# Two mixing layers: the heads' projections first, then pooling and gating, with values, gates and pooled part as one 400-column moving operand

## The chip, the cores and the metric

The kernel runs on one core of one Trainium2 chip. The time is device microseconds of one execution; three executions of the kernel before give a median of 1850.83 us. Smaller is better. All arithmetic is float32 in accuracy: every large product is made of three matmuls on float32r operands (high part by high part, high by low, low by high).

## The reference, cut to what matters

Two blocks of two layers each act on 256 tokens of 1024 channels. The change concerns the mixing half of the two layers of the second block, where `l` is 0 and 1:

```
h = rms_norm_2(x, norm_mix_pre[l])
z = h @ w_in[l]
za, zq, zkv, zg, zc, zd = split(z)          # 512, 256, 384, 12, 512, 256 columns
y_conv = conformer_conv(za, ...)            # gate, 31 taps along time, layer norm, silu
y_nsa  = nsa_attention(zq, zkv, sigmoid(zg), ...)   # 4 heads: compressed, selected, window branches
y_sgu  = spatial_gating(zc, ...)            # gelu, layer norm of v, 128x128 mixing along time, u * f
y_pool = multiscale_pool(zd, ...)           # running means minus the value, a small projection
y = concat(y_conv, y_nsa, y_sgu, y_pool) @ w_out[l]
x = x + rms_norm_2(y, norm_mix_post[l])
```

The four parts are independent of each other until `w_out`, whose 1024 rows fall into four groups of 256: rows 0 for the convolution, 1 for the heads, 2 for the gating, 3 for the pooled part.

## The kernel before, in words

One Python function writes the instruction stream of each engine in a fixed order. While it does so it keeps a model clock for each engine; small generators (one for each chain such as the pooled part or a pair of heads) are advanced between stretches of matmuls, and each next instruction of a chain is written when the model says that its inputs will be there. On the chip each engine takes its instructions in the order written. So what is written behind a matmul that waits, waits too.

Weights come as chunks of 1 MB or 0.5 MB (512 KB is one unit, 128 x 1024) over SyncE's queue in the order of `_plan()`, into four raw buffers (`wraw`). ScalarE casts each unit to `whi`, VectorE subtracts to make `wlo`; there are seven unit buffers. `MIX_ORDER` (line 57) is the order in which a mixing layer's projections run, and also the order of its chunks in `_weights`. `MIX_ROWS` (line 58) is the order of the four groups of rows of `w_out`.

In `mix` (line 2113) the order is: `begin`, which multiplies the first two pairs of units (`ag0`, `ag1`, the convolution's input) by the not yet scaled input while the norm is made, after which `make_h` writes the scaled input `hh`, `hl` in eight chunks of 128 channels (order 0, 2, 1, 3, 4, 6, 5, 7); then

- `v` (48 matmuls with tokens as stationary operand and 256 weight columns moving) and `u` (48 matmuls of the other form), the two halves of the gating, each followed by a gelu on ScalarE; a generator `sgu_gen` makes the layer norm, the mixing along time and the product;
- `conv`, which waits until `gated_input` has written the convolution's second input half, and then makes 18 of its 31 taps on TensorE, while 31 taps of the first half and 13 of the second run on VectorE as fillers, wherever VectorE's model clock is less than 1 us behind;
- `cvf` and `kk` (24 matmuls each: compressed keys and values; the other keys), `cw1` (the compression), `q` (48 matmuls);
- `cvt` (48: values and 12 gate columns, padded with 116 zero columns to 256) and `zd` (48: the pooled part), then `pool_gen`;
- `mm4`, which takes four neighbouring PSUM banks, and the four groups of rows, 48 matmuls each, in the order 2, 3, 0, 1. Before each group `rows` waits until its part is in `oh`, `ol`.

Two generators `nsa_heads` (t = 0, 1) each do two heads: logits, masked maximum on VectorE, exponentials on ScalarE, scaling on VectorE, transposes on TensorE, copies to `PT` on ScalarE, value products. Both use the same `P` and `PT` buffers. `self.busy` keeps the second from its logits until the first has its value products written. `tokens` (line 841) and `unit` (line 832) are the two forms of projection. After the fourth group `post` makes the norm, and the convolutional feed-forward layer (`ffn2`) follows.

Of the kernel before, what the change touches and what calls it, by code (L numbers as in the profile page):

```python
# [24 lines left out]
F32 = mybir.dt.float32  # L25
# [4 lines left out]
OP = mybir.AluOpType  # L30
# [23 lines left out]

FOX_ORDER = '0 1 f v0 2 3 v1 4 5 v2 6 7 v3'.split()

MIX_ORDER = 'v u conv cvf kk cw1 q cvt zd'.split()
MIX_ROWS = (2, 3, 0, 1)


DIL_TOKENS = ((3, 3, 3), (3, 3, 3), (3, 3, 3), (1, 1, 3))
# [6 lines left out]
def _weights(seg):  # L68

    kind, l, j = seg  # L70
    out = []
    if kind in ("ffn", "ffn2"):
        if kind == "ffn":
            g, u, d = (("ffn_w_gate", (l, j)), 0), (("ffn_w_up", (l, j)), 0), ("ffn_w_down", (l, j))
        else:
            g, u, d = (("ffn_up_2", (l,)), 0), (("ffn_up_2", (l,)), 2816), ("ffn_down_2", (l,))
        for t in range(FT):
            out.append((("pair", g[0], g[1] + t * 128, u[0], u[1] + t * 128), 2))
            if t % 2 and t > 4:
                out.append((("row", d, (t // 2 - 2) * 256), 2))  # L80
        for half in range(2):
            out.append((("last", d, half), 2))
    elif kind == "fox":
        w = ("fox_w_in", (0,))
        for i in FOX_ORDER:
            out.append((("one", w, 3072, 16), 1) if i == "f" else
                       (("tok", w, 2048 + int(i[1]) * 256) if i[0] == "v" else
                        ("pair", w, int(i) * 128, w, 1024 + int(i) * 128), 2))
        for c in range(4):
            out.append((("row", ("fox_w_out", (0,)), c * 256), 2))  # L90
    elif kind == "dil":
        w = ("dil_w_in", (0,))
        for c in range(4):
            toks = [(("tok", w, (g * 3 + 2) * 1024 + c * 256), 2) for g in range(3)]
            qk = [(("pair", w, o, w, o + 1024), 2) for e in range(2) for g in range(3) for o in (g * 3072 + (2 * c + e) * 128,)]
            early = 0 if c else 2
            out += qk[:early] + toks[:DIL_TOKENS[c][0]]
            for e in range(2):
                out += qk[max(3 * e, early):3 * e + 3]
                out += toks[DIL_TOKENS[c][e]:DIL_TOKENS[c][e + 1]]  # L100
        for c in range(4):
            out.append((("row", ("dil_w_out", (0,)), c * 256), 2))
    elif kind == "mix":
        for which in ["ag0", "ag1"] + [w for w in MIX_ORDER if w != "conv"]:
            n = 1 if which in ("cvf", "kk") else 2
            out.append((("cw1", l) if which == "cw1" else ("mixt" if which in ("v", "cvt", "zd") else "mix", l, which), n))
        for c in MIX_ROWS:
            out.append((("row", ("w_out_2", (l,)), c * 256), 2))
    return out
# [75 lines left out]
def _chunk_data(key, a):  # L185

    kind = key[0]
    tok = lambda w: np.concatenate([_kxn(w[:512]), _kxn(w[512:])], axis=1)
    get = lambda m: a[m[0]][m[1]]
    if kind == "mod":  # L190
        _, l, b = key
        return a["mod_w"][l][:, b * 128:(b + 2) * 128].T.reshape(2, 128, 1024).transpose(1, 0, 2).reshape(128, -1)
    if kind == "pair":
        _, m0, c0, m1, c1 = key
        return np.concatenate([_kxn(get(m0)[:, c0:c0 + 128]), _kxn(get(m1)[:, c1:c1 + 128])], axis=1)
    if kind == "wave":
        _, i, part = key
        r = slice(i * 256, i * 256 + 256)
        gu = [get(("ffn_w_" + n, (0, 0)))[r] for n in ("gate", "up")]
        return np.concatenate([_kxn(np.concatenate([m[:, t * 128:t * 128 + 256] for m in gu], axis=1))  # L200
                               for t in ((0, 2), (4, 6))[part]], axis=1)
    if kind == "one":
        _, m, c0, n = key
        w = get(m)[:, c0:c0 + n]
        return _kxn(np.concatenate([w, np.zeros((w.shape[0], 128 - n), np.float32)], axis=1))
    if kind == "tok":
        _, m, c0 = key
        return tok(get(m)[:, c0:c0 + 256])
    if kind == "row":
        _, m, r0 = key  # L210
        w = get(m)[r0:r0 + 256]
        return np.concatenate([_kxn(w[:, :512]), _kxn(w[:, 512:])], axis=1)
    if kind == "last":
        _, m, half = key
        w = get(m)[-512:, half * 512:half * 512 + 512]
        return np.concatenate([_kxn(w[:256]), _kxn(w[256:])], axis=1)
    if kind in ("mix", "mixt"):
        _, l, which = key
        cols = _mix_columns(which)
        real = [c for c in cols if c is not None]  # L220
        w = a["w_in_2"][l][:, real]
        if len(real) < len(cols):
            w = np.concatenate([w, np.zeros((1024, len(cols) - len(real)), np.float32)], axis=1)
        if kind == "mixt":
            return tok(w)
        return np.concatenate([_kxn(w[:, i:i + 128]) for i in range(0, w.shape[1], 128)], axis=1)
    _, l = key
    return np.concatenate([a[n][l].reshape(32, 64, 64).transpose(1, 0, 2).reshape(64, -1)
                           for n in ("nsa_ck_w1_2", "nsa_cv_w1_2")], axis=0)
# [163 lines left out]
NRAW = 4  # L393
NU = 7
UNIT = 1024


def parted(ap):
# [153 lines left out]
class Stream:  # L552
# [42 lines left out]
    def step(self, limit, later=None):  # L595


        i, u = self.at
# [12 lines left out]
        if key[0] == "mod":  # L611
            col = key[1] * 72 + key[2] + u
            nc.vector.tensor_tensor_reduce(src, src, k.cb, 1.0, 0.0, OP.mult, OP.add, k.modr[:, col:col + 1])
        else:
            if self.live >= limit:
                return False
            self.live += 1
            hi = k.whi.tile([128, UNIT], F32R, name="whi", bufs=NU)
            lo = k.whi.tile([128, UNIT], F32R, name="wlo", bufs=NU)
            nc.scalar.copy(hi, src)  # L620
            low = lambda: nc.vector.tensor_tensor(lo, src, hi.bitcast(F32), op=OP.subtract)
            if later is None:
                low()
            else:
                later.append(low)
            self.units.append((key, u, hi, lo))
# [13 lines left out]
    def get(self, *check):  # L640
        find = lambda: next((i for i, x in enumerate(self.units) if x[0][:len(check)] == check), None)
        while find() is None:
            assert self.step(NU), ("stuck", self.at)
        key, u, hi, lo = self.units[find()]
        del self.units[find()]
        kind = key[0]
        if kind == "cw1":
            return hi
        r = {"row": ("p (k n) -> p k n", 2), "last": ("p (k n) -> p k n", 2), "wave": ("p (k n) -> p k n", 2), "tok": ("p (k n) -> p k n", 4), "mixt": ("p (k n) -> p k n", 4)}
        f, n = r.get(kind, ("p (k n) -> p k n", 8))  # L650
        return hi.rearrange(f, k=n), lo.rearrange(f, k=n)

# [17 lines left out]
class K:  # L670
# [1309 lines left out]
    def nsa_heads(self, t, q, qr, kr, vt, kc, vc, gates, pvs):  # L1980
# [7 lines left out]
        nm, sm, cf = self.small(12, "nm"), self.small(12, "sums"), self.small(12, "cf")  # L1988
        cm = self.c("causal")

        while self.busy:
            yield
        self.busy.add(0)
        yield from self.on("pe", qr, kr, kc)
# [39 lines left out]
        for e in range(2):  # L2034
            c = cf[:, 6 * e:6 * e + 6]
            for o, n, i in ((768, 15, 0), (0, 128, 1), (128, 256, 4)):
# [4 lines left out]
                    continue  # L2041
                p = P[e][:, :768].rearrange("p (b n) -> p b n", b=2)[:, :, o:o + n]
                nc.vector.tensor_tensor(p, p, c[:, i:i + 2][:, :, None].to_broadcast([128, 2, n]), op=OP.mult)
        for e in range(2):
            pT = PT[:, e * 1024:e * 1024 + 1024]
            yield from self.on("pe", P[e])
# [13 lines left out]
            nc.scalar.copy(pT[:, 512:768], T2[:, 0:256])  # L2060
            nc.scalar.copy(pT[:15, 768:1024], T2[:15, 256:512])
            self.rel(T2)
        yield from self.on("pe", PT)
        pv = yield from self.bank()
        x = PT.rearrange("p (e n) -> p e n", e=2)
# [2 lines left out]
        for e in range(2):  # L2068
            nc.tensor.matmul(pv[64 * e:64 * e + 64, :S], vc, PT[:15, e * 1024 + 768:e * 1024 + 1024], start=False, stop=True,
                             skip_group_check=True)  # L2070
        self.busy.remove(0)
        pvs[t] = pv
        yield from self.o_store(pvs, 2 * t, 2 + t)
        if t:
# [38 lines left out]
    def mix(self, l, norm, following):  # L2113
# [110 lines left out]
            self.wait(lambda: cmp)  # L2224
            self.st.free_raw()

        def cvt():
            pv = self.tokens("mixt", l, "cvt")
            ps = v3(pv)
            nc.scalar.copy(vt, ps[:, :, 0:128])  # L2230
            nc.scalar.activation(gates, ps[:, :, 128:140], AF.Tanh, scale=0.5)
            self.rel(pv)
            nc.vector.tensor_scalar(gates, gates, 0.5, 0.5, op0=OP.mult, op1=OP.add)
            nc.vector.tensor_tensor(gates[:, :, 0:12:3], gates[:, :, 0:12:3],
                                    self.c("valid")[:, :, None].to_broadcast([128, 2, 4]), op=OP.mult)
            ready.add("v")

        def rope_q(ps):
            yield from self.rope2_gen(qr, v3(q), v3(ps), 0.125, ps)
# [7 lines left out]
                self.pending.append((lambda: len(ready) == 3 and len(cmp) == 2,  # L2247
                                     self.nsa_heads(t, v3(q), qr, kr, vt, kc, vc, gates, pvs)))

        def zd():  # L2250
            ps = self.tokens("mixt", l, "zd")
            zt = self.t512("zt")
            nc.vector.tensor_copy(zt, ps)
            self.rel(ps)
            self.gens.append(store(self.pool_gen(l, zt), 3))

        f = {"v": v_, "u": u_, "conv": conv_products, "cvf": cvf, "kk": kk, "cw1": cw1, "cvt": cvt, "q": q_, "zd": zd}
        heads()
        for w in MIX_ORDER:
            f[w]()  # L2260
# [118 lines left out]
```

## Time and profile before

| | |
|---|---|
| three timed executions | 1848.05, 1850.83, 1851.8 us (median 1850.83) |
| the profiled execution: its own time | 1849.76 us |
| its span in the trace | 1848.0 us |
| TensorE, VectorE, ScalarE, GpSimd busy | 98%, 80%, 54%, 2% |
| mixing layer 0, from `begin` to the last matmul of the rows | 1217.97 to 1326.87 us |
| mixing layer 1, likewise | 1528.41 to 1640.26 us |

Between the span and the execution's own time lie 1.76 us that no instruction of the trace covers. Starts are microseconds from the span's start. A busy TensorE is not TensorE at its peak, because matmuls overlap: one of 256 columns is recorded as 0.28 us long, but the next starts 0.12 us after it. So the distance of starts is what a matmul costs here, and in the timeline a wait of TensorE shows as a larger distance.

### The profile page before, as it was taken

The page shows a single profiled execution, that of the slowest core. Times are in us where ns is not written, and L with a number is a line of the kernel's source. Part 1 is how long each engine was busy: PE and PEld are TensorE (multiplying, and loading weights), DVE is VectorE, ACT ScalarE, POOL GpSimd, SP SyncE. Part 2 cuts the span into 40 slices and gives each one's busy share as a digit, 9 for nine tenths or more (in the row PEclk, how much of TensorE's full clock was granted, in tenths as well). Part 3 has the DMA queues.
Part 4 walks back from the last instruction along what each step waited for, and adds up shares of the span by engine and source line. Part 5 has one row for each costly group of instructions (what it writes and reads, how often), then busy time and mean ns, then how long its engine had stood idle before and what let it go on. Part 6 is the DMA issues. An engine that isn't in the chain of part 4 may idle for free.

```text
span 1848.0 us, 36709 instructions
## 1 busy us (share of the span) xinstructions
PE 1801.9 (98%) x15239; PEld 1755.8 (95%) x15239; DVE 1479.2 (80%) x2696; ACT 1006.4 (54%) x1706; POOL 42.7 (2%) x51
## 2 busy tenths in 40 slices
PE   8999999999999999999999999999999999999997
PEld 7999999999999999999999999998899998889997
DVE  7978798898779867779788965589698779879876
ACT  4544568644454445555555654454676554566653
POOL 0200010000000000000000000000000000000000
PEclk9999999999999999999999999999999999999999
DMA  9889375499848973433333566533255543325550
GB/s 392 307 347 341 116 291 184 162 364 352 312 151 343 340 277 129 183 137 122 143 125 138 208 244 223 185 135 137 92 195 210 183 160 137 115 87 204 212 183 24
DMA packets 54474, 378.36 MB, mean 205 GB/s; under 512 B 6305, under 2 KB 7809, under 8 KB 9506
## 3 DMA queue, kind: packets, MB, share of 16 engines
q1 hardware_dynamic: 52992, 372.42, 54.5%
q0 software_dynamic: 1168, 3.46, 0.6%
q8 instruction: 119, 1.95, 0.4%
q14 instruction: 49, 0.40, 0.1%
q10 hardware_dynamic: 146, 0.14, 0.0%
HBM read 374.89 MB, written 1.05 MB: 203 GB/s over the span
## 4 chain that ended last, share of the span: by engine, by line
PE 67%; issue 18%; DVE 10%; ACT 5%; POOL 1%; DMA 0%; POOLq 0%; DVEq 0%; ACTq 0%
PE banks L427 67%; DVE ar L427 3%; DVE wlo L427 2%; ACT ar L427 1%; DVE x L427 1%; ACT whi L427 1%; POOL rz L427 1%; DVE sq L427 1%; DVE hl L427 1%; ACT L427 1%; ACT hh L427 1%; ACT sq L427 0%; DVE ht L427 0%; DVE rs L427 0%; DVE ol L427 0%
## 5 line engine op out<-in xcount | busy, mean ns | idle before, releaser
L427 DVE TENSOR_TENSOR wlo<-wraw,whi 128x1024 fp32r<-128x1024 f32 x557 | 669.8, 1220 | 173.8 <-ACT whi L427 172.8
L427 PE MATMUL banks<-hh,whi 128*128 128x256 f32 (+1 forms) x2792 | 792.2, 284 | 2.3 <-ACT whi L427 1.1
L427 PE MATMUL banks<-hh,wlo 128*128 128x256 f32 (+1 forms) x2792 | 782.4, 281 | 2.9 <-DVE wlo L427 2.9
L427 PE MATMUL banks<-hl,whi 128*128 128x256 f32 (+1 forms) x2792 | 782.2, 281 | 0.8 <-DVE hl L427 0.8
L427 ACT CAST whi<-wraw 128x1024 fp32r<-128x1024 f32 x557 | 569.4, 1048 | 181.6 <-DMA wraw<-w 93.4
L427 PEld LDWEIGHTS banks<-hh,whi 128*128 128x128 f32 x2792 | 525.6, 188 | 6.0 <-ACT hh L427 2.3
L427 PEld LDWEIGHTS banks<-hh,wlo 128*128 128x128 f32 x2792 | 526.0, 189 | 3.7 <-DVE wlo L427 3.7
L427 PEld LDWEIGHTS banks<-hl,whi 128*128 128x128 f32 x2792 | 526.4, 189 | 1.4 <-DVE hl L427 1.4
L427 PE MATMUL banks<-oh,whi 128*128 128x256 f32 x1312 | 372.7, 284 | 7.8 <-DVE x L427 3.5
L427 PE MATMUL banks<-ol,whi 128*128 128x256 f32 x1312 | 368.3, 281 | 4.0 <-DVE ol L427 3.8
L427 PE MATMUL banks<-oh,wlo 128*128 128x256 f32 x1312 | 367.7, 280 | 0.0
L427 PEld LDWEIGHTS banks<-oh,whi 128*128 128x128 f32 x1312 | 247.1, 188 | 15.6 <-DVE x L427 6.0
L427 PEld LDWEIGHTS banks<-ol,whi 128*128 128x128 f32 x1312 | 247.3, 188 | 4.9 <-DVE ol L427 4.9
L427 PEld LDWEIGHTS banks<-oh,wlo 128*128 128x128 f32 x1312 | 247.3, 188 | 0.0
L427 DVE CUSTOM_DVE_ANT_0 wraw<-wraw,cb 128x1024 f32<-128x1024 f32 x128 | 152.0, 1216 | 0.0
L427 ACT ACTIVATE sg<-banks 128x256 f32<-128x256 f32 x82 | 31.4, 384 | 163.9 <-PE banks L427 163.8
L427 PE MATMUL banks<-whi,hh 128*128 128x256 f32 x352 | 102.2, 290 | 1.6 <-ACT hh L427 1.4
L427 PE MATMUL banks<-whi,hl 128*128 128x256 f32 x352 | 99.1, 282 | 0.1
L427 PE MATMUL banks<-wlo,hh 128*128 128x256 f32 x352 | 98.8, 281 | 0.0
L427 DVE SCALAR_TENSOR_TENSOR cy<-cs,vec,cy 128x255 f32<-128x255 f32 (+1 forms) x176 | 83.7, 481 | 7.8 <-ACT cy L427 4.7
L427 DVE TENSOR_TENSOR sg<-banks,sg 128x256 f32<-128x256 f32 x82 | 34.4, 422 | 62.7 <-ACT sg L427 62.6
L427 ACT ACTIVATE cy<-cs,vec 128x256 f32<-128x256 f32 x88 | 47.9, 594 | 49.6 <-DVE cs L427 48.8
(214 smaller groups left out, 1734.1 us busy)
## 6 DMA issues: line engine op xcount, KB each, us to landing
wraw<-w SPq DMA_DIRECT2D x342, 1024.0 KB, 4.9
ar<-w SPq DMA_DIRECT2D x8, 1024.0 KB, 9.1
wraw<-w SPq DMA_DIRECT2D x5, 512.0 KB, 3.3
ar<-lw POOLq DMA_DIRECT2D x2, 752.0 KB, 5.1
x<-x SPq DMA_DIRECT2D x2, 512.0 KB, 4.8
out<-x SPq DMA_DIRECT2D x8, 128.0 KB, 1.9
ar<-bands POOLq DMA_DIRECT2D x1, 544.0 KB, 8.1
ar<-dm POOLq DMA_DIRECT2D x1, 512.0 KB, 9.1
```

Source lines behind the costliest of these rows:

```text
L427: return f(out, *args, **kw)
```

## The change

The order of a mixing layer becomes `cvf kk conv cw1 q cz v u`, and that of the rows 3, 2, 0, 1. `cvt` and `zd` become one step `cz`: its weights are two chunks `mixz` of two units (the same bytes as before); a unit holds two k-chunks of 512 columns, of which 144 (values, gates, 4 zero columns) and 256 (pooled part) are used, so that one matmul has 400 moving columns. It writes two neighbouring PSUM banks, one for each half of the tokens. Cast and subtraction of such a unit take 800 of the 1024 columns. The heads' lock is split in two: lock 0 for `P` is given back after the transposes, lock 1 for `PT` is taken before them and given back after the value products.

```diff
-MIX_ORDER = 'v u conv cvf kk cw1 q cvt zd'.split()
-MIX_ROWS = (2, 3, 0, 1)
+MIX_ORDER = 'cvf kk conv cw1 q cz v u'.split()
+MIX_ROWS = (3, 2, 0, 1)
...
+            if which == "cz":
+                out += [(("mixz", l, part), 2) for part in range(2)]
+                continue
...
+    if kind == "mixz":
+        _, l, part = key
+        w = np.zeros((512, 512), np.float32)
+        rows = a["w_in_2"][l][part * 512:part * 512 + 512]
+        cvt = [c for c in _mix_columns("cvt") if c is not None]
+        w[:, :len(cvt)] = rows[:, cvt]
+        w[:, 144:400] = rows[:, _mix_columns("zd")]
+        return _kxn(w)
...
+CZ = 400
...
-            nc.scalar.copy(hi, src)
-            low = lambda: nc.vector.tensor_tensor(lo, src, hi.bitcast(F32), op=OP.subtract)
+            part = lambda t: t.rearrange("p (k n) -> p k n", k=2)[:, :, :CZ] if key[0] == "mixz" else t
+            nc.scalar.copy(part(hi), part(src))
+            low = lambda: nc.vector.tensor_tensor(part(lo), part(src), part(hi.bitcast(F32)), op=OP.subtract)
...
-        while self.busy:
+        while 0 in self.busy:
             yield
         self.busy.add(0)
...
+        while 1 in self.busy:
+            yield
+        self.busy.add(1)
         for e in range(2):
             pT = PT[:, e * 1024:e * 1024 + 1024]
...
             self.rel(T2)
+        self.busy.remove(0)
         yield from self.on("pe", PT)
...
-        self.busy.remove(0)
+        self.busy.remove(1)
         pvs[t] = pv
...
-        def cvt():
-            pv = self.tokens("mixt", l, "cvt")
-            ps = v3(pv)
+        def cz():
+
+            self.wait(lambda: self.can(2))
+            ps = self.take(self.can(2))
+            for kk in range(8):
+                if kk % 2 == 0:
+                    w = self.st.get("mixz", l, kk // 4)
+                for tt in range(2):
+                    s = slice(tt * 128, tt * 128 + 128)
+                    self.mm3(ps[:, tt, :CZ], self.hh[:, kk, s], self.hl[:, kk, s], w[0][:, kk % 2, :CZ], w[1][:, kk % 2, :CZ],
+                             kk == 0, kk == 7)
+                if kk % 2:
+                    self.st.free()
+                self.step()
             nc.scalar.copy(vt, ps[:, :, 0:128])
             nc.scalar.activation(gates, ps[:, :, 128:140], AF.Tanh, scale=0.5)
-            self.rel(pv)
+            zt = self.t512("zt")
+            nc.vector.tensor_copy(v3(zt), ps[:, :, 144:400])
+            self.rel(ps)
...
             ready.add("v")
+            self.gens.append(store(self.pool_gen(l, zt), 3))
...
-        def zd():
-            ps = self.tokens("mixt", l, "zd")
-            zt = self.t512("zt")
-            nc.vector.tensor_copy(zt, ps)
-            self.rel(ps)
-            self.gens.append(store(self.pool_gen(l, zt), 3))
```

## Rows read from the trace of the kernel before

**Rows 1.** The page: busy time of each engine, and two groups of instructions.

```profile
PE 1801.9 (98%) x15239; PEld 1755.8 (95%) x15239; DVE 1479.2 (80%) x2696; ACT 1006.4 (54%) x1706; POOL 42.7 (2%) x51
...
L427 DVE TENSOR_TENSOR wlo<-wraw,whi 128x1024 fp32r<-128x1024 f32 x557 | 669.8, 1220 | 173.8 <-ACT whi L427 172.8
```

**Rows 2.** Layer 0 by stretch: length, busy PE, PEld, DVE, ACT, POOL, clock, DMA.

```profile
1231.00:1242.30 11.30, 11.30 (x97) 11.30 (x96) 10.58 (x27) 7.79 (x11) 0.00 (x0) 1.00 0.48 186
...
1290.70:1306.30 15.60, 12.92 (x89) 10.40 (x86) 7.90 (x26) 10.15 (x18) 0.00 (x0) 0.78 0.19 69
...
1315.50:1320.50 5.00, 4.60 (x39) 3.18 (x37) 3.89 (x7) 2.20 (x6) 0.00 (x0) 1.00 0.60 210
```

**Rows 3.** The same view, mixing layer 1.

```profile
1605.80:1619.50 13.70, 10.13 (x88) 7.85 (x86) 7.70 (x26) 9.72 (x18) 0.00 (x0) 1.00 0.22 78
```

**Rows 4.** Timeline of TensorE, layer 0, pooled rows: start, duration, engine, instruction.

```profile
1291.10 1.03 PE L427 MATMUL banks<-pb,ar 128*128 128x256 f32 x4
1293.71 0.38 PE L427 MATMUL banks<-oh,whi 128*128 128x256 f32 x1 [1.58 <-ACT oh L427]
1295.19 0.58 PE L427 MATMUL banks<-ol,whi 128*128 128x256 f32 x1 [1.10 <-DVE ol L427]
...
1301.25 2.11 PE L427 MATMUL banks<-ar 128*64 128x256 f32 x20
```

**Rows 5.** Timeline of TensorE, layer 1, the same place.

```profile
1606.23 1.03 PE L427 MATMUL banks<-pb,ar 128*128 128x256 f32 x4
1608.83 0.38 PE L427 MATMUL banks<-oh,whi 128*128 128x256 f32 x1 [1.58 <-ACT oh L427]
1610.32 0.39 PE L427 MATMUL banks<-ol,whi 128*128 128x256 f32 x1 [1.10 <-DVE ol L427]
...
1613.57 2.11 PE L427 MATMUL banks<-ar 128*64 128x256 f32 x20
...
1618.32 0.93 PE L427 MATMUL banks<-kr,qr 64*128 64x128 f32 x8 [0.89 <-DVE ol L427]
```

**Rows 6.** Timeline of TensorE, layer 0: first of the 48 of `v`, first after them.

```profile
1230.93 0.28 PE L427 MATMUL banks<-whi,hh 128*128 128x256 f32 x1
...
1236.62 0.28 PE L427 MATMUL banks<-hh,whi 128*128 128x256 f32 x1
```

**Rows 7.** Timeline of VectorE, layer 0: ends of the chains.

```profile
1231.80 0.42 DVE L427 TENSOR_TENSOR hl<-ht,hh 128x256 fp32r<-128x256 f32 x1 [0.21 <-ACT hh L427]
...
1236.74 0.75 DVE L427 SCALAR_TENSOR_TENSOR ar<-sg,gy 128x256 f32<-128x256 f32 x2
...
1247.61 0.68 DVE L427 TENSOR_TENSOR ol<-sy,oh 128x512 fp32r<-128x512 f32 x1
...
1283.55 0.41 DVE L427 TENSOR_TENSOR ar<-ar,banks 128x256 f32<-128x256 f32 x1
...
1285.96 0.68 DVE L427 COPY zt<-banks 128x512 f32<-128x512 f32 x1
...
1303.81 0.69 DVE L427 TENSOR_TENSOR ol<-cs,oh 128x512 fp32r<-128x512 f32 x1 [1.76 <-ACT oh L427]
```

**Rows 8.** Timeline of VectorE, layer 1: last `hl`, and the convolution's inputs.

```profile
1549.10 0.42 DVE L427 TENSOR_TENSOR hl<-ht,hh 128x256 fp32r<-128x256 f32 x1 [0.19 <-ACT hh L427]
...
1552.91 0.75 DVE L427 SCALAR_TENSOR_TENSOR ar<-sg,gy 128x256 f32<-128x256 f32 x2
```

**Rows 9.** Timeline of TensorE, layer 1: first matmul after the 48 of `v`.

```profile
1550.98 0.28 PE L427 MATMUL banks<-hh,whi 128*128 128x256 f32 x1
```

**Rows 10.** Timeline of ScalarE, layer 0: table load, first and last of 24 exponential records.

```profile
1277.76 1.28 ACT L427 ACT_TABLE_LOAD   x1 [1.74 <-DVE nm L427]
1279.06 0.40 ACT L427 ACTIVATE ar<-ar,nm 128x128 f32<-128x128 f32 x1
...
1283.65 0.19 ACT L427 ACTIVATION_READ_ACCUMULATOR ar<-ar,nm 128x1 f32 x1
```

**Rows 11.** Groups of ScalarE's instructions, mixing layer 0 (busy, mean ns, idle).

```profile
L427 ACT ACT_TABLE_LOAD x4 | 5.1, 1283 | 2.5 <-DVE nm L427 1.7 <-PE banks L427 0.7
```

More of the change, by code (lines that the diff above doesn't have):

```diff
@@ L648, in get @@
             return hi
-        r = {"row": ("p (k n) -> p k n", 2), "last": ("p (k n) -> p k n", 2), "wave": ("p (k n) -> p k n", 2), "tok": ("p (k n) -> p k n", 4), "mixt": ("p (k n) -> p k n", 4)}
+        r = {"row": ("p (k n) -> p k n", 2), "last": ("p (k n) -> p k n", 2), "wave": ("p (k n) -> p k n", 2), "mixz": ("p (k n) -> p k n", 2), "tok": ("p (k n) -> p k n", 4), "mixt": ("p (k n) -> p k n", 4)}
         f, n = r.get(kind, ("p (k n) -> p k n", 8))
@@ L2248, in heads @@
                                      self.nsa_heads(t, v3(q), qr, kr, vt, kc, vc, gates, pvs)))
-        def zd():
-            ps = self.tokens("mixt", l, "zd")
-            zt = self.t512("zt")
-            nc.vector.tensor_copy(zt, ps)
-            self.rel(ps)
-            self.gens.append(store(self.pool_gen(l, zt), 3))
-        f = {"v": v_, "u": u_, "conv": conv_products, "cvf": cvf, "kk": kk, "cw1": cw1, "cvt": cvt, "q": q_, "zd": zd}
+        f = {"v": v_, "u": u_, "conv": conv_products, "cvf": cvf, "kk": kk, "cw1": cw1, "cz": cz, "q": q_}
         heads()
```

## The prediction, made before the changed kernel had been run

> **What bounds the kernel now.** I read four views in this order. The page first: TensorE is busy for 98% of the span [rows 1], so the time falls by what is taken out of TensorE's stream, or out of its waits, and by little else. VectorE at 80% is the next engine, and the reader should not take that average for slack: then come the stretches. In the first projections of mixing layer 0 TensorE is busy for all 11.30 us and VectorE for 10.58 of them [rows 2]; both are full there. In the stretch where the rows begin, TensorE is busy for 12.92 of 15.60 us and its granted clock is 0.78 on average, so it fell part of the time from 2.4 to 1.2 GHz. Layer 1 has the same gap at full clock, 10.13 of 13.70 us [rows 3].
>
> Third, the timeline of that gap. The four matmuls of the pooled part's projection start at 1291.10; at 118 ns each they are through at 1291.57, yet the next start is at 1293.71, released by ScalarE's `oh`, and the one after at 1295.19, released by VectorE's `ol` [rows 4]. The pooled part is the last projection and its rows come second, so its chain has only one group of rows to hide behind. All that is written behind these rows (the first heads' transposes, the value products, and with them the second heads' logits) stands behind them too, since an engine keeps the order written. Layer 1 shows the same two waits, and one more of 0.89 us by the profile before the second heads' logits [rows 5].
>
> Fourth, I followed the chains that end in `oh`/`ol` backwards through the timelines of VectorE and ScalarE; they stand where the parts below use them.
>
> **The change part by part.**
>
> *The waits at the pooled rows.* Layer 0: 1293.71 - 1291.57 = 2.14; 1295.19 - (1293.71 + 0.12) = 1.36; and the stretch from there to the value products, 1301.25 - 1295.19 = 6.06, has the same instructions as layer 1's 1613.57 - 1610.32 = 3.25, at half the clock: 2.81 more. Sum 6.3 [rows 4, 5]. Layer 1: 2.13 and 1.37 likewise, and about 1.0 before 1618.32: sum 4.5. Together 10.8 us. Afterwards the pooled chain starts at the end of `cz`, with `v` and `u` behind it, 2 x 5.69 = 11.4 us of matmuls [rows 6]. Today the chain takes from 1285.96 (`zt`) to about 1295.1 (where its `ol` releases TensorE), 9.2 us, two of them its own wait [rows 4, 7]. So it is covered, with some 2 us to spare, and I take the whole 10.8 as gone. If the cover fails, the wait comes back.
>
> *The wide operand.* `v`'s 48 matmuls take 1236.62 - 1230.93 = 5.69 us, 118.5 ns each for 256 columns at a granted clock of 1.00 [rows 2, 6]. `cvt` and `zd` are 96 of these, 11.4 us. The trace has no float32r matmul of 400 columns. If everything scales with the columns it takes 118.5 x 400/256 = 185 ns; if each further column costs one cycle of 2.4 GHz, 118.5 + 144 x 0.417 = 178; two old ones would be 237. I take 180: of the 118.5 ns, 106.7 are 256 cycles of 2.4 GHz and grow with the columns, and the other 12 belong to the instruction as far as the row can tell. 48 x 0.180 = 8.6, so 2.7 us per layer, 5.5 in all; between 0 (237 ns) and 5.7 (178). The page TensorE: Matmul & The Clock Gate of the Trainium skill (Back-to-back issue gap) gives N/2.4 + 2.5 ns, an estimate of 109 for 256 and 169 for 400 columns; by it the gain would be 4.7 us, but the trace shows 118.5 for 256 [rows 6], so the rule misses some 9 ns per matmul here. Casts and subtractions of four units become 22% shorter (1220 ns each on VectorE, so 1.1 us per layer [rows 1]); VectorE is hidden behind TensorE where it happens, so nothing.
>
> *Layer 1's start.* `make_h` ends there at 1549.10 + 0.42 = 1549.52 [rows 8], and the first step follows its pace. `cvf` has three matmuls per chunk of channels against six in `v`, so its last three cannot start before 1549.5 and it ends at 1549.9; with `kk`, 48 matmuls are done at 1552.7. In the kernel before, `v`'s 48 end with 1550.98, where `u` begins [rows 9]. Cost 1.7 us; between 1 and 2.5. Layer 0 pays nothing: the last `hl` is there at 1232.2, and `cvf` comes to it at 1230.93 + 21 x 0.1185 = 1233.4 [rows 6, 7].
>
> *The convolution moves forward.* It now follows 48 matmuls and not 96. In layer 0 it would start at 1236.6; its second input half is written until 1236.74 + 0.75 = 1237.5 [rows 7]. In layer 1, 1552.7 against 1553.7 [rows 8]. I take 0.9 us in each, 1.8. Lower bound 0 (three subtractions of 1.2 us stand ahead of it on VectorE and could be written later), upper bound 2.5 each, if the additions behind `cvf` come first. Behind the waiting matmuls stands `cw1`, which has its input by then.
>
> *New waits at the rows.* Group 3 is ready. Group 2 (gating) is the new risk: from the end of `u` (96 matmuls after 1230.93, 1242.3) its chain takes until 1248.3, 6.0 us [rows 6, 7]; cover is group 3, 5.7, and the gating's own 16 matmuls, 1.1. Group 0 (convolution): today its taps end with 1283.55, and `ol` follows at 1304.5, 21 us later, much of that behind the waiting TensorE [rows 7]. VectorE's work in the layer stays, in a shorter time; the taps are fillers and give way to heads that now come ahead of two projections, 11.4 us earlier. Between 0 and 4 us per layer; I take 1, so 2.0. The split lock lets the second heads' logits go ahead of the first heads' value products (2.1 us [rows 4]); it earns only if the last group waits for them, and in the last stretch TensorE is idle 0.40 of 5.00 us [rows 2], so 0 to 0.8; I take 0.4 for each layer.
>
> *Order of the chunks.* The same bytes in the same queue; half-MB chunks come first, while the convolution uses none. DMA's share is 0.48 in that stretch [rows 2]: nothing. Without that cover the price is a unit's time on TensorE, half of 5.69 us. GpSimd, which clears the compression's buffer, does it earlier; it is busy 2% [rows 1].
>
> Sum: -10.8 - 5.5 - 0.8 + 1.7 + 1.8 + 2.0 = -11.6 us. The profiled execution took 1849.76 us, span and ends together, so 1838.2; the median lies 1.07 above it: **1839 us**.
>
> **The rivals.** *All waits go* (no new wait at rows or convolution, -10.8 - 5.7 - 0.8 + 1.0 = -16.3, and the small waits of the compression too, up to 3): 1832 to 1835. For it: the kernel before fills TensorE wherever a chain has more cover than length.
>
> *The convolution's rows wait instead*, 4 us per layer and 2.5 at its start: -10.8 - 5.5 + 1.7 + 5 + 8 = -1.6, so 1849; with 2 us per layer at the rows, 1845. For it: VectorE has 10.58 of 11.30 us filled [rows 2]. Against: after the projections it has 7.90 of 15.60.
>
> *400 columns cost as much as two of 256*: -11.6 + 5.5, so 1845. No row speaks for it.
>
> *Slower: gating behind the exponentials.* The first heads' exponentials take ScalarE from 1279.06 to 1283.84, 4.8 us, after a table load of 1.28 [rows 10]. They now fall among `v` and `u`, whose gelu needs another table: 4 loads per layer [rows 11] become 5 to 7. If the exponentials are written just ahead of `u`'s gelu, group 2 is late by 4.8 + 2 x 1.28 - 0.8 = 6.6 us; if the clock then falls as in layer 0 now, 2.8 more. Twice 9.4, so -11.6 + 18.8 = +7.2: 1858. It decides from 5.8 us per layer. Against: logits come right after `cz`, and from there to the end of `u` are 11.4 us [rows 6], nearly twice what load and exponentials take. The Trainium skill's ScalarE: Activation LUTs (What ACT_TABLE_LOAD costs) adds about 1.38 us of draining to each switch, which would make two switches 5.3 us and the wait 9.3; here the first exponential starts 1.30 us after the load's start [rows 10], so no draining shows behind it.
>
> **How the numbers follow.** Forecast 0.55 (1835 to 1843); all waits go 0.20; convolution's rows wait 0.13, of which 0.05 within 0.2%; wide operand earns nothing 0.05; gating behind the exponentials 0.07, of which a little comes out even. 0.2% is 3.7 us, about what a measurement of this kernel can tell from no change. Faster: 0.55 + 0.20 + 0.08 + 0.04 = 0.87; same 0.07; slower 0.06. The range from 1830 to 1847 leaves out the slower case, the worst of the convolution's, and a little below.
>
> **What would show it.** 96 matmuls with 400 moving columns in place of 192 with 256, starting 178 to 185 ns apart; no wait of TensorE for `oh`/`ol` at the first group of rows, and the clock at 1.00 throughout layer 0's rows; `cvf` of layer 1 in pace with `hl`; a wait of about 1 us before the convolution. I am wrong if a group of rows waits over 4 us for VectorE's or ScalarE's last step, above all group 2 with exponentials just ahead of the gelu, or group 0 with taps still running when `u` ends.

## The result, and the profile after

The changed kernel takes 1867.66 us (median of 4 runs, 1866.34 to 1868.72) against 1850.53 for the kernel before on the same chip: a ratio of 1.0093, 95% interval 1.008 to 1.0105. It is 17 us slower; forecast were 11.6 us less. The slower side had a chance of 0.06; the rival "gating behind the exponentials" had 0.07 and gave 1858.

The page of the changed kernel, span and busy time of each engine, against [rows 1]:

```profile
span 1864.6 us, 36515 instructions
PE 1806.0 (97%) x15143; PEld 1757.5 (94%) x15143; DVE 1477.9 (79%) x2696; ACT 1010.3 (54%) x1710; POOL 42.7 (2%) x51
```

TensorE has fewer instructions and is still busy for 1806 us: busy time counts matmuls at half clock as long ones. So go by stretches. First the changed kernel (layer 0's and layer 1's rows, layer 1's start), then the same stretches of the kernel before (layer 1's start last); columns are the stretch, its length, busy time of PE, PEld, DVE, ACT, POOL, granted clock, DMA share, GB/s.

```profile
1285.90:1332.00 46.10, 39.98 (x306) 35.59 (x305) 27.64 (x82) 26.23 (x60) 0.00 (x0) 0.89 0.33 115
1547.20:1560.60 13.40, 10.49 (x53) 9.05 (x53) 11.90 (x27) 7.37 (x15) 0.79 (x1) 0.75 0.23 79
1608.90:1656.80 47.90, 39.47 (x305) 34.27 (x305) 27.45 (x82) 26.24 (x59) 0.00 (x0) 0.86 0.31 110
```

```profile
1283.10:1326.90 43.80, 40.65 (x319) 35.88 (x318) 26.52 (x82) 26.86 (x66) 0.00 (x0) 0.92 0.27 97
1598.20:1640.30 42.10, 38.01 (x319) 33.38 (x318) 26.54 (x82) 26.68 (x66) 0.00 (x0) 1.00 0.28 101
1544.10:1556.70 12.60, 12.34 (x97) 11.76 (x98) 12.21 (x31) 6.80 (x13) 0.00 (x0) 1.00 0.39 152
```

The rows take 2.3 and 5.8 us longer than before, although the pooled part's two waits [rows 2 to 5] lay in that stretch and are gone. (From the norm's sums to the end of the rows the two layers take 110.2 and 112.1 us, where they took 104.7 and 100.8: 16.8 us more, nearly the whole difference.) Layer 1's rows ran at full clock before and now at 0.86. TensorE's timeline in layer 0 shows what came instead (start, duration, instruction, idle time before it and its releaser):

```profile
1285.91 0.28 PE L439 MATMUL banks<-oh,whi 128*128 128x256 f32 x1
...
1301.93 0.28 PE L439 MATMUL banks<-oh,whi 128*128 128x256 f32 x1
1307.18 0.45 PE L439 MATMUL banks<-ol,whi 128*128 128x256 f32 x1 [4.97 <-DVE ol L439]
1307.43 0.42 PE L439 MATMUL banks<-oh,wlo 128*128 128x256 f32 x1
1307.64 0.42 PE L439 MATMUL banks<-oh,whi 128*128 128x256 f32 x1
...
1308.42 3.24 PE L439 MATMUL banks<-ar 128*64 128x256 f32 x20
```

The pooled rows start at 1285.91 with no wait. The second group, gating, waits 4.97 us for VectorE's `ol`, and what follows starts 0.21 us apart, at half clock, until about 1310.7. The first heads' value products (1308.42) stand behind it. Layer 1 has the same, in two waits:

```profile
1623.99 0.38 PE L439 MATMUL banks<-oh,whi 128*128 128x256 f32 x1 [1.73 <-ACT oh L439]
1629.68 0.58 PE L439 MATMUL banks<-ol,whi 128*128 128x256 f32 x1 [5.30 <-DVE ol L439]
```

Back from that `ol` in layer 0: ScalarE's timeline, then VectorE's.

```profile
1294.38 1.28 ACT L439 ACT_TABLE_LOAD   x1
1295.68 0.40 ACT L439 ACTIVATE ar<-ar,nm 128x128 f32<-128x128 f32 x1
...
1300.13 0.29 ACT L439 ACTIVATE ar<-ar,nm 128x15 f32<-128x15 f32 x1
1300.33 0.19 ACT L439 ACTIVATION_READ_ACCUMULATOR ar<-ar,nm 128x1 f32 x1
1300.81 0.62 ACT L439 CAST oh<-sy 128x512 fp32r<-128x512 f32 x1 [0.29 <-DVE sy L439]
1301.34 1.05 ACT L439 CAST whi<-wraw 128x1024 fp32r<-128x1024 f32 x1
```

```profile
1299.17 0.88 DVE L439 SCALAR_TENSOR_TENSOR sy<-banks,vec,ar 128x256 f32<-128x256 f32 x2 [1.31 <-PE banks L439]
1300.08 0.69 DVE L439 TENSOR_TENSOR sy<-sy,su 128x512 f32<-128x512 f32 x1
1300.69 1.22 DVE L439 TENSOR_TENSOR wlo<-wraw,whi 128x1024 fp32r<-128x1024 f32 x1
1302.42 1.23 DVE L439 TENSOR_TENSOR wlo<-wraw,whi 128x1024 fp32r<-128x1024 f32 x1 [0.51 <-ACT whi L439]
1303.56 0.22 DVE L439 RECIPROCAL cf<-sums 128x12 f32<-128x12 f32 x1
...
1305.51 1.02 DVE L439 TENSOR_TENSOR ar<-ar,cf 128x256 f32<-128x256 f32 x2
1306.44 0.69 DVE L439 TENSOR_TENSOR ol<-sy,oh 128x512 fp32r<-128x512 f32 x1
```

Gating's product `sy` is there at 1300.77, `oh` at 1301.43, but `ol` starts at 1306.44: two unit subtractions and 2.9 us of scaling are written ahead of it. The exponentials (1295.68 to 1300.5) and the scaling (1303.56 to 1306.4) are those of the second pair of heads, whose logits the split lock let through. At this point I suspected, beside the lock, the first heads' exponentials, behind which gating's first gelu starts 4.6 us after its matmuls' end (1283.11 against 1278.48, a table load of 1.28 included), and VectorE's first scaling.

### The profile page after: what moved, and what is told of

The parts are those of the page before. It is cut to its first block, busy times and chain, and to the rows that moved or that the text cites. A ratio compares the mean times of both kernels' runs of the same rounds, so it can differ in the third digit from the quotient of the medians.

```text
span 1864.6 us, 36515 instructions
## 1 busy us (share of the span) xinstructions
PE 1806.0 (97%) x15143; PEld 1757.5 (94%) x15143; DVE 1477.9 (79%) x2696; ACT 1010.3 (54%) x1710; POOL 42.7 (2%) x51
## 4 chain that ended last, share of the span: by engine, by line
PE 65%; issue 18%; DVE 11%; ACT 4%; POOL 1%; DMA 0%; POOLq 0%; DVEq 0%; ACTq 0%
PE banks L439 65%; DVE ar L439 4%; DVE wlo L439 2%; DVE x L439 1%; ACT ar L439 1%; DVE hl L439 1%; ACT whi L439 1%; POOL rz L439 1%; DVE sq L439 1%; ACT L439 1%; ACT hh L439 1%; DVE ht L439 1%; ACT sq L439 0%; DVE gy L439 0%; DVE wraw L439 0%
## 5 line engine op out<-in xcount | busy, mean ns | idle before, releaser
L439 DVE TENSOR_TENSOR wlo<-wraw,whi 128x1024 fp32r<-128x1024 f32 (+1 forms) x557 | 668.6, 1218 | 182.3 <-ACT whi L439 181.4
L439 ACT CAST whi<-wraw 128x1024 fp32r<-128x1024 f32 (+1 forms) x557 | 569.1, 1045 | 158.9 <-PE banks L439 87.1
L439 PEld LDWEIGHTS banks<-ol,whi 128*128 128x128 f32 x1312 | 248.2, 189 | 12.5 <-DVE ol L439 12.5
L439 PE MATMUL banks<-whi,hh 128*128 128x256 f32 (+1 forms) x320 | 95.9, 300 | 0.0
L439 PE MATMUL banks<-whi,hl 128*128 128x256 f32 (+1 forms) x320 | 92.0, 287 | 0.0
L439 PE MATMUL banks<-wlo,hh 128*128 128x256 f32 (+1 forms) x320 | 91.9, 287 | 0.0
```

Source lines behind the costliest of these rows:

```text
L439: return f(out, *args, **kw)
```

## The experiments

Each kernel is described against the changed kernel or the one before; all are compared with the kernel before on their own chip.

**1. The wide operand alone.** Order, rows and lock as before, `cz` in place of `cvt zd`.

```
-MIX_ORDER = 'cvf kk conv cw1 q cz v u'.split()
-MIX_ROWS = (3, 2, 0, 1)
+MIX_ORDER = 'v u conv cvf kk cw1 q cz'.split()
+MIX_ROWS = (2, 3, 0, 1)
-        while 0 in self.busy:
+        while self.busy:
...
-        while 1 in self.busy:
-            yield
-        self.busy.add(1)
```

> The wide operand alone: 400 columns for the pooled part, values and gates, but the old order of projections (values and gating first), the old order of rows and the old lock. Theory (the new order makes the waits at gating's rows; the wide operand is innocent): 48 matmuls of 182 ns in place of 96 of 118.5, so 2.6 us less per layer and 5.3 in all; up to 3 us of it is lost where the first heads' logits now come after all of the wide projection. About 1845 us, 1845 to 1851. Rival (two banks taken at once, or the wide matmuls, cost the time): 1855 us or more, with a wait at the wide projection.

1859.21 us, ratio 1.0054 (1.0039 to 1.0069): slower by about 9.6 us. That is in the rival's range, but the wait that the rival asked for is not there: TensorE does not stand still at the wide projection, and only in layer 1 do the rows behind it wait 1.60 us, by the profile for `zt`, VectorE's copy out of its banks. The projections became shorter, but the heads start only after all of `cz`, where before they had `zd` as cover, and at the end nothing is left to cover them. TensorE's timeline of layer 0:

```profile
1319.15 0.44 PE L439 MATMUL banks<-cst,ar 128*128 128x128 f32 x1 [6.77 <-DVE ar L439]
```

That is the second heads' transposes waiting for their scaling; layer 1 has the same wait with 5.63 us. So I put the loss down to the heads' lateness and not to the width. I had put that lateness at 3 us over both layers, and the two waits alone make 12.4.

**2. The order alone.** New orders on the kernel before, with `cvt zd` separate and the old lock.

```
-MIX_ORDER = 'v u conv cvf kk cw1 q cvt zd'.split()
-MIX_ROWS = (2, 3, 0, 1)
+MIX_ORDER = 'cvf kk conv cw1 q cvt zd v u'.split()
+MIX_ROWS = (3, 2, 0, 1)
```

> The order alone: compression, keys and convolution first, values and gating last, pooled rows first, with the two separate projections of 256 columns and the old lock. Theory (the order makes the waits): as slow as the changed kernel and the 5.3 us of the wide operand more, about 1873 us, 1866 to 1880, with group 2's rows waiting for VectorE's ol by over 3 us in each layer. Rival (the order is innocent, the width or the split lock costs): 1848 to 1852 us.

1866.45 us, ratio 1.0094 (1.0079 to 1.0109). The order without wide operand and split lock loses as much as the whole change. Here the heads are ready at `cvt`, a projection earlier; the first pair's value products (1287.34) are written among the matmuls of `u`, so even the old lock lets the second pair's logits (1289.37) and softmax go ahead of gating's last steps. ScalarE's timeline: the second heads' exponentials stand ahead of `u`'s gelu, whose matmuls ended at 1293.46.

```profile
1290.98 1.28 ACT L427 ACT_TABLE_LOAD   x1
1292.27 0.40 ACT L427 ACTIVATE ar<-ar,nm 128x128 f32<-128x128 f32 x1
...
1297.07 1.28 ACT L427 ACT_TABLE_LOAD   x1
1298.37 0.60 ACT L427 ACTIVATE su<-banks 128x512 f32<-128x512 f32 x1
```

Gating's rows then wait 1.2 us for `oh` and 2.2 for `ol` in each layer, less than the 3 that the theory asked of `ol`; in layer 0 the second heads' transposes wait 1.80 us for their scaling before that. How the loss divides between these was not tested.

**3. The convolution's rows second.**

```
-MIX_ROWS = (3, 2, 0, 1)
+MIX_ROWS = (3, 0, 2, 1)
```

> The changed kernel with one thing altered: the convolution's rows stand between the pooled part's and gating's. Theory (gating's chain is late and has only one group of rows as cover): 5.7 us more cover in each layer, so the waits of 5.0 and 7.0 us at gating's rows go, and with them the half clock around them: 1846 to 1858 us. Rival (TensorE stalls at whatever group comes second, because VectorE is late with everything): the wait moves to the convolution's rows, and the time stays at 1864 to 1869 us.

1853.63 us, ratio 1.002 (1.001 to 1.0029): 14 us won back with one more group as cover. Layer 0's rows fall to 38.8 us, layer 1's to 42.1; a wait of 1.6 to 1.7 us for gating's `ol` is left in each layer.

**4. The old lock.** The changed kernel with the second heads' logits kept back until the first heads' value products are written.

```
-        while 0 in self.busy:
+        while self.busy:
...
-        while 1 in self.busy:
-            yield
-        self.busy.add(1)
```

> The changed kernel with the old single lock: the second heads' logits come only after the first heads' value products. Theory (the split lock lets the second heads' exponentials and scalings be written ahead of gating's last steps, and so is a part of its lateness): the wait at gating's rows shrinks by 2 to 4 us per layer, and some comes back at the heads' end: 1858 to 1866 us. Rival (the lock is innocent; the table switches and the first heads' scalings make gating late): 1866 to 1870 us, with the same wait at gating's rows.

1848.14 us, ratio 0.9993 (0.9984 to 1.0002): 19.5 us less than the changed kernel (1.0% by the two ratios), twice what I gave the lock at most, and no longer to be told from the kernel before. The two stretches of rows (columns as above):

```profile
1287.30:1324.60 37.30, 35.88 (x307) 31.81 (x306) 27.20 (x82) 25.86 (x60) 0.00 (x0) 1.00 0.39 142
...
1603.20:1639.40 36.20, 35.37 (x304) 31.64 (x305) 26.13 (x76) 24.82 (x57) 0.00 (x0) 1.00 0.39 146
```

8.8 and 11.7 us shorter than with the split lock, at full clock. ScalarE now casts `oh` before it loads the table for the exponentials, and VectorE's `ol<-sy` starts 5.8 us sooner than at 1306.44, or 7.2 us sooner when both are counted from the start of their rows (1287.30 and 1285.91):

```profile
1298.19 0.62 ACT L439 CAST oh<-sy 128x512 fp32r<-128x512 f32 x1
...
1299.78 1.28 ACT L439 ACT_TABLE_LOAD   x1
```

```profile
1300.64 0.69 DVE L439 TENSOR_TENSOR ol<-sy,oh 128x512 fp32r<-128x512 f32 x1
```

The first heads' exponentials still stand ahead of gating's first gelu here, and in neither layer do gating's rows wait for `oh` or `ol`. My suspicion of them falls.

**5 and 6. Which part of the second heads does it.** Split lock kept; the second heads wait ahead of their exponentials (5), or only ahead of their scaling (6).

```
+        while t and 2 not in self.stored:
+            yield
         for e in range(2):
             yield from self.on("act", P[e])            # 5: here
...
+        while t and 2 not in self.stored:
+            yield
         yield from self.on("dve", sm)                  # 6: here instead
```

> The changed kernel, split lock and all, but the second heads' exponentials (and with them their scaling) are held back until gating's last step is written. The second heads' logits stay where the split lock put them. Theory (the lock harms only because the second heads' softmax is written ahead of gating's last steps on ScalarE and VectorE): as good as the old single lock, 1846 to 1853 us, and no wait over 2 us at gating's rows. Rival (the logits themselves on TensorE, the table switches or the first heads' scaling do it): 1860 us or more.

> The changed kernel, but only the second heads' scaling on VectorE is held back until gating's last step is written: on VectorE, ol<-sy now stands ahead of 2.9 us of scaling and of the wait for the last exponential's sum; ScalarE's order, exponentials ahead of oh<-sy, is as in the changed kernel. Theory A (VectorE's order is most of it): ol<-sy starts some 5 us earlier in each layer, the waits of 5.0 and 5.3 us go and part of the half clock with them: 1850 to 1857 us. Theory B (ScalarE's exponentials ahead of oh<-sy are most of it): 1860 to 1866 us, the wait is now for oh.

1858.0 us (ratio 1.0046, 1.0031 to 1.0061) and 1859.32 (1.0053, 1.0038 to 1.0068). Each wins back about half of the 19.5 us; neither theory's range holds 5, and 6 lies between A and B. In 6 gating's rows wait for both, 1.74 us for `oh` and 2.42 for `ol` in layer 0: `ol<-sy` starts only 2.9 us earlier (1303.58), because a unit's subtraction ahead of it waits for a cast that stands behind the exponentials on ScalarE. VectorE's timeline of 5 shows what is left there:

```profile
1299.04 0.69 DVE L439 TENSOR_TENSOR sy<-sy,su 128x512 f32<-128x512 f32 x1
1299.65 1.22 DVE L439 TENSOR_TENSOR wlo<-wraw,whi 128x1024 fp32r<-128x1024 f32 x1
1302.93 1.23 DVE L439 TENSOR_TENSOR wlo<-wraw,whi 128x1024 fp32r<-128x1024 f32 x1 [2.07 <-ACT whi L439]
1304.08 0.42 DVE L439 TENSOR_TENSOR ol<-banks,oh 128x256 fp32r<-128x256 f32 x1
1304.41 0.68 DVE L439 TENSOR_TENSOR ol<-sy,oh 128x512 fp32r<-128x512 f32 x1
```

The logits still stand ahead of gating's mixing matmuls on TensorE (from 1292.33 to 1295.04, 2.7 us), and their masked maximum ahead of gating's `sy` on VectorE (from 1295.54 to 1298.14, 2.6 us). Behind them a unit's subtraction, which waits for its cast on ScalarE, is written ahead of `ol`. TensorE's rows wait 2.75 us for that `ol`.

**7. The split lock on the kernel before.** The four places of the lock as in the diff of the change; nothing else differs from the kernel before.

> The kernel before with the split lock alone; in layer 0 its instructions keep their order, in layer 1 the second heads' logits come ahead of the rows and the value products. Theory (the split lock harms only where gating's last steps are still to be written; here gating is done long before the heads): 1846 to 1852 us, no more than the 0.9 us that layer 1's second logits wait now to be won. Rival (the split lock costs some 8 to 10 us in any layer whose order it changes, by the second logits' place on TensorE): 1856 us or more.

1849.96 us, ratio 1.0001 (0.9992 to 1.0011). With gating first in the layer the lock costs nothing, and earns nothing either.

**8. The width in the new order.** As in 2, with `zd` ahead of `cvt`:

```
+MIX_ORDER = 'cvf kk conv cw1 q zd cvt v u'.split()
```

> The new order with two separate projections of 256 columns and the old lock, but the pooled part's projection ahead of that of values and gates, so that the heads become ready after both, as with the wide operand. Against the changed kernel with the old lock (1848.1 us) it differs by the wide operand alone. Theory (width is worth 96 x 118.5 - 48 x 182 ns = 2.6 us a layer, and the order of heads and gating sets the rest): 1853.4 us, 1851 to 1856. Rival (separate projections in the new order are bad whatever comes first, as the 1866.5 us with the opposite order of the two suggest): 1862 us or more.

1860.62 us, ratio 1.0061 (1.0046 to 1.0076): neither. Against the 1848.14 us of experiment 4 the width is worth 12.5 us here; in experiment 1 it cost 9.6. Three unit subtractions stand ahead of gating's `sy` in layer 0 (3.49 us on VectorE), and gating's rows wait 1.11 us for `oh` and 1.81 for `ol`. I read this as the width having no price of its own apart from its matmuls: it moves what is written around the heads. No run shows that, since none has both widths with everything else in the same places.

**9. The second heads held back altogether.** Split lock kept.

```
-        while 0 in self.busy:
+        while 0 in self.busy or t and 2 not in self.stored:
             yield
```

> The changed kernel, split lock kept, but the second heads start (logits, exponentials, scaling) only once gating's last step is written. Theory (the place of the second heads against gating's chain is all that the lock changes; the 10 us that holding the exponentials alone left were the second logits ahead of gating's matmuls on TensorE, and gating's ol behind unit casts that came later): all of it comes back, 1847 to 1850 us. Rival (a part of the lock's cost has nothing to do with gating): 1853 us or more.

1848.12 us, ratio 0.9993 (0.9984 to 1.0003): the time of experiment 4 again, with the lock still split. So the 19.5 us are the place of the second heads, from their logits on, against gating's chain; the split lock as such costs nothing that these runs can tell. Held back from the exponentials on (5), they give 9.7 us back, and the logits with their maximum make the rest.

**10 to 12. Layer 1's start.** All with the old lock; only `MIX_ORDER` differs.

```
+MIX_ORDER = 'cz cvf kk conv cw1 q v u'.split()     # 10
+MIX_ORDER = 'cz conv cvf kk cw1 q v u'.split()     # 11
+MIX_ORDER = 'v cvf kk conv cw1 q cz u'.split()     # 12
```

> The wide projection first of all (cz cvf kk conv cw1 q v u), pooled rows first, old lock: the 1848.1 us kernel with its first step changed. Theory (layer 1's start loses 4.4 us because cvf has three matmuls per chunk of channels, cannot fill TensorE while the chunks arrive, and the clock halves; six matmuls of 182 ns per chunk can): of the 5.6 us that the first 48 matmuls and the wait for the convolution's input take too long in layer 1, 4 to 5.6 come back, and up to 1.5 us in layer 0: 1841 to 1845 us. Rival (the heads now become ready 8.7 us earlier against the convolution, and VectorE is full there; what is won at the start is lost behind it): 1848 us or more.

> As the previous kernel, with the convolution right behind the wide projection (cz conv cvf kk cw1 q v u), which puts the convolution some 8.7 us of TensorE behind the first matmul, where its input should be there. Theory: the start as good as in the previous kernel, the taps may begin 5.7 us earlier: 1840 to 1846 us. Rival (convolution's input is not there after 8.7 us and TensorE waits as it does now): the previous kernel's time and 2 to 5 us.

> Gating's v first and its u last (v cvf kk conv cw1 q cz u), pooled rows first, old lock. Theory on layer 1's start: v has six matmuls per chunk too, so the 4 to 5.6 us come back there as with the wide projection; gating's layer norm and first gelu leave the crowded end. But only u stands between the wide projection and the rows, 5.7 us against a pooled chain of 9: a wait of up to 3 us per layer at the pooled rows. 1842 to 1849 us. Rival (heads late as in the order alone or the width alone): 1855 us or more, with the second heads' transposes waiting at the end of the rows.

1846.67 us (ratio 0.9986, 0.9977 to 0.9996), 1860.33 (1.0057, 1.004 to 1.0074) and 1866.67 (1.0095, 1.008 to 1.011). The first is the best kernel of the study, by 0.14%, though its interval overlaps that of experiment 4; its time lies between its theory and its rival. 11 is slower than both of its ranges. 12 has its rival's time but not its sign: what waits is not the second heads' transposes. In 10, layer 1 won at the start (from the norm's sums to the convolution 22.7 us with 48 matmuls more, against 16.0 in experiment 4; those 48 alone take 8.7, and 16 small matmuls of the pooled part that now lie there 1.1, so some 3 us came back, where 4 to 5.6 were expected) and lost in the rows, 48.3 us against 37.0 in its own layer 0:

```profile
1603.44 0.93 PE L439 MATMUL banks<-kr,qr 64*128 64x128 f32 x8 [3.17 <-DVE cz L439]
...
1607.78 0.58 PE L439 MATMUL banks<-oh,whi 128*128 128x256 f32 x1 [2.83 <-ACT oh L439]
```

There the convolution's layer norm (`cz` here is its tile, not the projection) is written between gating's layer norm and its product. In 12 the same chain is in the way in both layers (3.74 and 4.4 us), and gating's rows wait behind it; layer 0:

```profile
1297.47 1.35 PE L439 MATMUL banks<-cst,cz 128*128 128x128 f32 x4 [3.74 <-DVE cz L439]
1301.10 0.58 PE L439 MATMUL banks<-oh,whi 128*128 128x256 f32 x1 [2.28 <-ACT oh L439]
1304.65 0.58 PE L439 MATMUL banks<-ol,whi 128*128 128x256 f32 x1 [2.97 <-DVE ol L439]
```

What made 11 slow I did not follow up. TensorE's compression matmuls start 3.08 and 3.60 us late in its two layers, and the profile names no releaser; in both, VectorE's additions that make their input start only 0.9 us before them (1258.52 and 1576.48), behind convolution taps and a unit's subtraction, so they are the likely cause, not shown. The rows wait as well, 3.2 us for `oh` and `ol` in layer 0 and 3.9 for `ol` in layer 1.

## Why the prediction was wrong, point by point

**The step that failed** is the split lock within "new waits at the rows": "it earns only if the last group waits for them ... I take 0.4 for each layer". It costs 9.8 us in each on average (1867.66 - 1848.14 = 19.5; experiments 4 and 9). I asked who would wait for the second heads' logits, and not what their logits, exponentials and scalings would be written ahead of. With gating last, that is gating's last steps. So the length of gating's chain failed with it. I took 6.0 us for it from the kernel before, against a cover of 5.7 + 1.1, and so no wait at group 2; in layer 0 it takes 21.2 us from the end of `u` (1285.91) to the end of `ol` (1307.13). With the old lock it is still 14.0 us (1287.29 to 1301.33), but there the first heads' value products and the second heads' logits stand ahead of gating's rows on TensorE and cover it. The 1 us for each layer, with 4 as bound, was taken for new waits at group 0, the convolution; the wait is at group 2, 5.0 and 7.0 us, and the clock comes on top: 0.89 and 0.86 over 46 and 48 us.

**The rival "gating behind the exponentials"** had the place and the victim right, and the wrong heads. It let the first heads' exponentials fall ahead of `u`'s gelu. In the changed kernel those fall ahead of `v`'s gelu, and experiment 4, which has them too, shows no wait at gating's rows. The second heads' do the harm, on ScalarE, and also on VectorE and by their logits on TensorE, where the rival had no term. Against it I had said that the logits come 11.4 us ahead of `u`'s end: true of the first pair alone.

**Pooled rows:** right. No wait at 1285.91 or in layer 1 (1608.85). With the old lock the rows stretch is 43.8 - 37.3 = 6.5 us shorter than before in layer 0, 42.1 - 36.2 = 5.9 in layer 1, near the 6.3 and 4.5 of the forecast, though some other work changed sides of that border too (319 matmuls recorded there before, 307 and 304 after).

**The wide operand:** its matmul is right. Six of 400 columns start 0.18 to 0.19 us apart (forecast 180 ns, 118.5 for 256):

```profile
1257.43 0.35 PE L439 MATMUL banks<-whi,hh 128*128 128x400 f32 x1
1257.62 0.35 PE L439 MATMUL banks<-wlo,hh 128*128 128x400 f32 x1
1257.80 0.35 PE L439 MATMUL banks<-whi,hl 128*128 128x400 f32 x1
```

By the formula that the Trainium skill (TensorE: Matmul & The Clock Gate, Back-to-back issue gap) gives for the isolated gap, N/2.4 + 2.5 ns, the estimate is 169 ns. The trace does not agree with that, by some 15 ns. What I left out is that a merged projection makes the heads wait for all of it (experiment 1).

**Layer 1's start and the convolution:** the place is right, the size too small, and it is the convolution's term that was mis-sized. From the layer's first matmul to the convolution it takes 27.0 us; the kernel before takes 28.3 with 48 matmuls more, 22.6 without their 5.69 [rows 6]: 4.4, forecast 1.7 + 0.9 = 2.6. TensorE is through with `cvf` and `kk` at about 1559.1 and then waits 1.33 us for VectorE, whose timeline has:

```profile
1554.28 0.43 DVE L439 TENSOR_TENSOR hl<-ht,hh 128x256 fp32r<-128x256 f32 x1 [0.19 <-ACT hh L439]
...
1556.96 1.65 DVE L439 TENSOR_TENSOR ar<-banks,ar 64x240 f32<-64x240 f32 x4
1558.64 0.43 DVE L439 SCALAR_TENSOR_TENSOR ar<-sg,gy 128x256 f32<-128x256 f32 x1
1558.98 1.22 DVE L439 TENSOR_TENSOR wlo<-wraw,whi 128x1024 fp32r<-128x1024 f32 x1
1560.12 0.42 DVE L439 SCALAR_TENSOR_TENSOR ar<-sg,gy 128x256 f32<-128x256 f32 x1
```

The additions behind `cvf` (1.65 us) stand ahead of the convolution's input, and a subtraction between its halves: the case that the forecast named for its upper bound of 2.5 us. From the end of the last `hl` to the convolution it is 5.88 us, where the kernel before had its input after 4.1 [rows 8]. Layer 0 has the same 5.88 us and the same wait of 1.33 us, at full clock, and paid 1.5 in place of 0.9. In layer 1 the clock was at 0.75 on average in the stretch shown above, with starts 213 ns apart until 1556.5, where the kernel before, with six matmuls of `v` for each chunk, ran at 1.00. That cost nothing here, since TensorE had to wait for VectorE anyway: in experiment 4 the clock fell for a shorter time (0.89 over this layer's start), TensorE waited longer (2.05 us), and the convolution again came 5.89 us behind the last `hl`.

**The sum without the lock:** 1848.1 against 1839 + 0.8. Of the 8 us that are missing, 1.8 are layer 1's start, 0.6 layer 0's, and about 1.7 the convolution of layer 1, which in the profiled execution of experiment 4 began at half clock (50.0 us from there to the rows, 48.3 in layer 0). The other 4 us stay open: waits of under 1 us each stand there (in layer 0 the compression's gelu 0.7, the convolution's layer norm 0.8, the copies of transposes 0.7), and none was tested.

## What to carry to other kernels

When a change lets a step start earlier on an in-order engine, list what it is now written ahead of, on every engine that the step's whole chain uses; its gain is bounded by who waits for it, its cost by who stands behind it. A chain that has moved to the end of a stage should have its last steps written first, and a lock that looked like mere caution may be what keeps that order. Before a group of rows is put second, count the groups ahead of it against the length of its chain with everything that may be written into it: here one more group (experiment 3) was worth 14 of the 17 us.

## What the runs showed of the hardware

A wait of 5.0 us in TensorE's stream was followed by matmuls 213 ns apart instead of 118 (layer 0, from 1307.4 to about 1310.7, granted clock 0.50), so it cost about 1.7 us more than its length. In layer 1 the two waits of 1.73 and 5.30 us were followed by half clock from 1629.7 to about 1638.4, which cost some 4.4 us more.

The clock did not follow from the waits alone. In layer 0 the changed kernel and experiment 3 have the same matmuls in the same order until the second group of rows begins, with the same two short waits (0.33 and 0.77 us against 0.31 and 0.77), and a stretch of 8.5 us behind the second one ran at 0.61 in the one and at 1.00 in the other. First the changed kernel, then experiment 3:

```profile
1291.90:1300.40 8.50, 8.38 (x52) 7.32 (x53) 7.15 (x32) 8.47 (x32) 0.00 (x0) 0.61 0.38 124
```

```profile
1291.80:1300.30 8.50, 8.14 (x75) 7.33 (x76) 8.47 (x33) 8.47 (x32) 0.00 (x0) 1.00 0.32 126
```

By the start of the second group the fall had put TensorE 2.8 us behind (the 49th matmul of the rows starts at 1301.93, in experiment 3 at 1299.09), most of which its wait for `ol` then took up: `ol<-sy` starts at 1306.44 in the one and at 1305.94 in the other. In the changed kernel's layer 1 the clock did not fall at this place. What sets it off I did not test.
